# First product of a block of seven copied into a second PSUM bank, output projection's low halves on VectorE

## The chip, the cores and the metric

The kernel runs on one core of a Trainium2 chip. The metric is the device time of one execution, in microseconds, as the median of several. The engines are PE (TensorE, matrix products), DVE (VectorE), ACT (ScalarE), POOL (GpSimd) and SP (SyncE, which here only issues transfers). Each works through its own queue in order.

## The reference

Two layers of a trunk in which three branches run side by side on 640 tokens (512 sample, 128 prompt) of width 1024, with an adaptive modulation ahead of them. Cut to the part that the change touches:

```python
mod = jax.nn.silu(cvec) @ w_mod + b_mod
shift, scale, gate = jnp.split(mod[:, None, :], 3, axis=-1)
h = rms_norm(x, norm_g) * (1 + scale) + shift
... = jnp.split(h @ w_in, split_at, axis=-1)          # fu, fz and gl among them
...                                                   # o_r, o_m, o_f: retention, attention, Fourier
branches = jnp.stack([o_r * silu(rz), o_m * silu(mz), o_f * silu(fz)], axis=2)
proj = jnp.einsum('btnw,nwd->btnd', branches, w_branch)
merged = jnp.sum(proj * jax.nn.sigmoid(gl.reshape(B, T, N_BRANCH, D_MODEL)), axis=2)
x = x + gate * (merged @ w_out)
```

All inputs and outputs are float32.

## The kernel before

**Numbers.** Every float32 operand is split into a high half, rounded by a cast on ACT, and a low half, the difference, taken by DVE or POOL. A product is made of three passes on PE: high by high, low by high, high by low. `split` does this, and `low` (L74) is the subtraction; the casts are L78. Weights come by DMA into `raw` (L92, two buffers, issued by SP), and `wload` casts and splits them. The names are the same throughout: `wh`, `wl` for weights, `hh`, `hl` for the activations, `bq` for a branch's output.

**Layout.** Activations lie with channels in the partitions and the 640 tokens in the free dimension, in two halves `a` and `b` of 320. One matrix product covers 128 x 128 weights and 128 x 320 activations.

**The product phase** (`ph0`, `ph1`, once a layer) makes the gates and the branch products. Its unit is `seven`: a 2 x 2 block product (two channel blocks by two token halves) by seven products of sums instead of eight. It has three PSUM banks' worth of accumulators A, C and, for the third product, B. In the order of the code: product 0 into A; ACT copies A into SBUF (L1117); product 2 into B, and DVE adds copy and bank (L1113), which is the first half of the first result; product 1 on top of A, copied (L1125); product 4 into C; product 3 on top of A, copied (L1131), and C added; then `rest`, which is put off until the next block's first copy: product 5 on top of A, which is consumed by `last`, and product 6 into C. A product that goes on top of A waits for the copy of A before it. For a gate the results go through a tanh (ACT, L1241 for the last one, L1245 for the others); for a branch DVE multiplies them by (gate + 1) (L1258, L1263) and adds them to the running sum `mg` (L1265). There are 21 such blocks a layer: the Fourier branch's SiLU gate, three times four gates, and two times four branches; the middle branch uses `four`, a plain block product, instead.

**PSUM.** Of eight banks the phase uses six in rotation as `bank`, one (`fill`) for the modulation products, and one (`po`) for their transposes.

**Between the bank products** PE does modulation products for later (L187, `fill<-mraw`): their weights `mraw` come by DMA (L175), whose issue stands in ACT's queue. `bql`, the low-pass part of a branch output, comes back through memory (`ofd`), and is cast at L78.

**The output projection** (`px0`, `px1`) follows. The merged sum is cast to `hh` (L81) and its low half `hl` taken on DVE (L82). `w_out` comes in eight tiles d = 0 to 7 of 128 x 1024; the low halves of d = 0 are taken on DVE, of the others on POOL; tiles 4 to 7 are called `xwh`, `xwl`. DVE evacuates each output product from PSUM (L1349). In layer 1 PE then transposes it (L1357), and ACT squares it (L1360).

**What sets the order.** The tile scheduler places each engine's instructions by a simulated time line. So a few instructions less on one engine move rows on all the others.

Of the kernel before, what the change touches and what calls it, by code (L numbers as in the profile page):

```python
# [14 lines left out]
P = 128  # L15
D = 1024
NK = 8
# [13 lines left out]
def build(nc, tc, A, O):  # L31
# [24 lines left out]
        return psum["p"].tile([P, 512], F32, name="sm", tag="sm", bufs=psum["nsm"])  # L56

    def bank():
        return psum["p"].tile([P, 512], F32, name="bank", tag="bank", bufs=6)[:, :320]

    def fillp():
        return psum["p"].tile([P, 512], F32, name="fill", tag="fill", bufs=1)
# [1034 lines left out]
        while tail:  # L1097
            tail.pop(0)()

    def seven(ws, xs, y1, y2, last, done, tick):  # L1100
        a, b = HALF

        def product(ps, i, first):
            n = len(xs[i])
            for k in range(n):
                w = ws[i][0][:, k, :], ws[i][1][:, k, :]
                x = xs[i][k]
                for j, (u, v) in enumerate(PASSES):
                    PE.matmul(ps, w[u], x[v], start=(first and k == 0 and j == 0), stop=(k == n - 1 and j == 2),  # L1109
                              skip_group_check=True)  # L1110

        def add(o, v, ps):
            DVE.tensor_tensor(o, ps, v, op=ALU.add)  # L1113

        A = bank()
        product(A, 0, True)
        ACT.copy(y1[:, a], A)  # L1117
        tick(0)
        flush()
        B = bank()  # L1120
        product(B, 2, True)
        add(y1[:, a], y1[:, a], B)
        tick(1)
        product(A, 1, False)
        ACT.copy(y2[:, a], A)  # L1125
        tick(2)
        C = bank()
        product(C, 4, True)
        tick(3)
        product(A, 3, False)  # L1130
        ACT.copy(y2[:, b], A)  # L1131
        add(y2[:, b], y2[:, b], C)
        tick(4)

        def rest():
            product(A, 5, False)
            last(A)
            done(0)
            tick(5)
            product(C, 6, False)  # L1140
            add(y2[:, a], y2[:, a], C)
            done(1)
            tick(6)

        tail.append(rest)
# [41 lines left out]
    for l in range(DEPTH):  # L1187
# [26 lines left out]
        with ExitStack() as s:  # L1214
            gp = pool(s, f"ga{l}")
            psum["s"].close()
            psum_pool(f"ph{l}")
            fillp(), pout()
            blocks = [(0, b) for b in range(8, 12)] + [(1, b) for b in range(8)] if l == 0 else [(1, b) for b in range(8, 12)]
            steps = mod_steps(blocks, gp)  # L1220
            next(steps)
# [7 lines left out]
                fourier_gate(off, j + 2, m)  # L1229
                nc.sync.dma_start(ofd[:, j + 2, :], o)  # L1230

            seven(w0, hq, *zs, lambda ps: ACT.copy(zs[0][:, b], ps), fourier_done, lambda i: None)
            bql = rp2.tile([P, 4, TT], F32R, name="bql", tag="of", bufs=1)

            def merge(d0, d1, hs=slice(0, TT)):
# [3 lines left out]
            def gates(y2, n, bq, parts, np_):  # L1239
                def last(ps):  # L1240
                    ACT.activation(y2[0][:, b], ps, AF.Tanh, scale=0.5)  # L1241

                def fin(j):
                    y = y2[j][:, a] if j == 0 else y2[j]
                    ACT.activation(y, y, AF.Tanh, scale=0.5)  # L1245

                def tick(i):
                    if i in (3, 6):
                        next(steps, None)
                    if i % 2 and len(bq) < np_:  # L1250
                        with tc.issue_after(gated.ins):
                            bq.append(next(parts))

                return last, fin, tick

            def products(y2, n, ms, ps):
                def last(acc):
                    DVE.scalar_tensor_tensor(ps[0][:, b], y2[0][:, b], 1.0, acc, op0=ALU.add, op1=ALU.mult)  # L1258

                def fin(j):  # L1260
                    y, m, p = y2[j], ms[j], ps[j]
                    s_ = a if j == 0 else slice(0, TT)
                    DVE.scalar_tensor_tensor(p[:, s_], y[:, s_], 1.0, p[:, s_], op0=ALU.add, op1=ALU.mult)  # L1263
                    if n:
                        DVE.tensor_tensor(m, m, p, op=ALU.add)  # L1265
                def tick(i):
                    if i in (3, 6):
                        next(steps, None)

                return last, fin, tick  # L1270

            for n, (idx, src, tmp) in enumerate(((1, omt, None), (0, ort, om), (2, ort, om))):
                if n:
# [4 lines left out]
                for i in range(4):  # L1278
                    if n and i % 2 == 0:
                        y2 = tmp[2:4]  # L1280
                    else:
                        y2 = [fl.tile([P, TT], F32, name="tg", tag="th", bufs=2) for _ in range(2)]
                    seven(gl_weights(wgp, l, C_GL + D * idx + 256 * i), hq, *y2, *gates(y2, n, bq, parts, np_))
                    if n == 2 and i == 3:
                        merge(0, 4)
                    if i == 0:
# [8 lines left out]
                        ends = (lambda: merge(4, 6), lambda j, hs: merge(6 + j, 7 + j, hs)) if (n, i) == (2, 3) else ()  # L1295
                        four(br_plain(l, idx, 256 * i), bq, y2, ms, ps, lambda i: next(steps, None) if i else None, *ends)
                    else:
                        seven(br_weights(wgp, l, idx, 256 * i), bq, *ps, *products(y2, n, ms, ps))
            merge(4, 6)
            flush()  # L1300
            merge(6, NK)
# [5 lines left out]
        with ExitStack() as s:  # L1307
# [9 lines left out]
            ws = []  # L1317
            for d in range(NK):
                view = rows(A["w_out"][l], 0, NK, P * d, P)
                eng = DVE if d == 0 else POOL  # L1320
                if d < 4:
                    ws.append(wload(view, NK, P, eng))
                else:
                    rv = wraw(view, NK, P)
                    w = tuple(xp.tile([P, NK, P], F32R, name=n, tag=n, bufs=4) for n in ("xwh", "xwl"))
                    split(*w, rv, leng=eng)
                    ws.append(w)

            def out_mm(d, a, b):
# [130 lines left out]
```

## Time and profile before

| | |
|---|---|
| median of 3 runs | 1473.63 us (1472.76 to 1474.07) |
| profiled execution | 1475.04 us, span 1473.3 us |
| granted clock, mean | 0.993 |
| PE busy | 1411.6 us, 96% of the span |
| DVE busy | 1025.5 us, 70% |
| ACT busy | 756.2 us, 51% |
| POOL busy | 239.1 us, 16% |
| DMA | 138.91 MB, mean 94 GB/s |

The product phase of layer 0 lies from about 430 to 700 us of the span, that of layer 1 from about 1150 to 1410; the output projections follow each. Busy time is the sum of an engine's instructions; matrix products overlap, so that the mean of one (0.31 us) is longer than the time from one to the next. "Granted clock" is the share of full speed that TensorE was given. The chain of waits follows the span back from its end, at each step to what released it. A wait is put down to the releaser that came last.

### The profile page before, as it was taken

How to read it: one execution, taken by the hardware profiler on the slowest of the kernel's cores; microseconds unless marked ns; L12 is line 12 of the kernel's file. 1: busy time of each engine (PE TensorE's matmuls, PEld its weight loads, DVE VectorE, ACT ScalarE, POOL GpSimd, SP SyncE). 2: the span in 40 equal slices, each digit the busy share in tenths (PEclk: the TensorE clock that was granted, in tenths of full speed). 3: DMA queues.
4: the chain of work that ended last, by engine and by line, in shares of the span. 5: the costliest groups of instructions: out<-in, count | busy, mean ns of one | idle time of the engine just before them, and what ended most of it. 6: DMA issues, size and time to landing. Idle time of an engine off the chain costs nothing.

```text
span 1473.3 us, 25184 instructions
## 1 busy us (share of the span) xinstructions
PE 1411.6 (96%) x9793; PEld 1345.2 (91%) x9793; DVE 1025.5 (70%) x1896; ACT 756.2 (51%) x1607; POOL 239.1 (16%) x227
## 2 busy tenths in 40 slices
PE   6999999999999999999999999999999999999997
PEld 4989989988988989999999899899889899999997
DVE  5367776666887686698573777765759778779843
ACT  5546666544545453455354566664545445445542
POOL 1220000301102211122312100021110112112240
PEclk9999999999999999999999999999999999999999
DMA  9520003331325474233532100042222433323342
GB/s 317 179 76 1 15 16 98 102 84 33 94 90 176 130 221 129 57 85 92 166 101 84 33 15 16 15 138 77 73 73 65 146 108 104 94 80 86 90 125 87
DMA packets 175847, 138.91 MB, mean 94 GB/s; under 512 B 8304, under 2 KB 168688, under 8 KB 175728
## 3 DMA queue, kind: packets, MB, share of 16 engines
q1 hardware_dynamic: 157680, 120.16, 28.1%
q10 hardware_dynamic: 18048, 17.15, 3.7%
q8 instruction: 77, 1.26, 0.4%
q14 instruction: 42, 0.34, 0.1%
HBM read 125.98 MB, written 11.30 MB: 93 GB/s over the span
## 4 chain that ended last, share of the span: by engine, by line
PE 74%; DVE 12%; DMA 5%; ACT 4%; issue 4%; POOL 1%; SPq 0%; POOLq 0%; ACTq 0%; DVEq 0%
PE bank L1109 25%; PE sm L85 6%; PE sm L87 5%; PE sm L86 5%; PE big L269 4%; PE bank L1080 4%; PE big L513 4%; PE fill L319 3%; PE sm L319 3%; PE sm L534 2%; PE sm L526 2%; DVE wl L74 2%; PE fill L187 2%; DMA raw<-in_w_in 1%; PE big L411 1%
## 5 line engine op out<-in xcount | busy, mean ns | idle before, releaser
L74 DVE TENSOR_TENSOR wl<-raw,wh 128x1024 fp32r<-128x1024 f32 (+5 forms) x146 | 153.8, 1055 | 87.3 <-ACT wh L78 39.0
L78 ACT CAST wh<-raw 128x1024 fp32r<-128x1024 f32 (+5 forms) x126 | 104.7, 833 | 86.2 <-DMA raw<-in_w_in 27.9
L1109 PE MATMUL bank<-hh,wh 128*128 128x320 f32 x416 | 130.0, 315 | 5.5 <-ACT tg L1125 4.4
L85 PE MATMUL sm<-wh,hh 128*128 128x256 f32 (+2 forms) x456 | 134.2, 295 | 0.5 <-DVE vl L74 0.5
L86 PE MATMUL sm<-wl,hh 128*128 128x256 f32 (+2 forms) x456 | 133.8, 294 | 0.0
L87 PE MATMUL sm<-wh,hl 128*128 128x256 f32 (+2 forms) x456 | 132.6, 294 | 0.0
L1109 PE MATMUL bank<-hl,wh 128*128 128x320 f32 x416 | 128.6, 310 | 0.0
L1109 PE MATMUL bank<-hh,wl 128*128 128x320 f32 x416 | 127.1, 311 | 0.0
L74 POOL TENSOR_TENSOR wl<-raw,wh 128x1024 fp32r<-128x1024 f32 (+1 forms) x32 | 66.4, 2075 | 294.9 <-ACT wh L78 215.7
L74 POOL TENSOR_TENSOR wl<-st,wh 128x512 fp32r<-128x512 f32 x26 | 38.0, 1463 | 328.8 <-ACT wh L78 328.8
L85 PEld LDWEIGHTS sm<-wh,hh 128*128 128x128 f32 x456 | 87.8, 193 | 2.2 <-issue 0.8
L1109 PEld LDWEIGHTS bank<-hh,wh 128*128 128x128 f32 x416 | 78.3, 188 | 11.9 <-ACT tg L1125 5.2
L86 PEld LDWEIGHTS sm<-wl,hh 128*128 128x128 f32 x456 | 87.8, 193 | 0.1
L87 PEld LDWEIGHTS sm<-wh,hl 128*128 128x128 f32 x456 | 87.4, 192 | 0.4 <-issue 0.4
L1109 PEld LDWEIGHTS bank<-hl,wh 128*128 128x128 f32 x416 | 78.5, 189 | 0.0
L1109 PEld LDWEIGHTS bank<-hh,wl 128*128 128x128 f32 x416 | 78.0, 189 | 0.0
L74 DVE TENSOR_TENSOR ptl<-sm,pth 128x384 fp32r<-128x384 f32 x128 | 67.2, 549 | 13.9 <-ACT pth L78 12.9
L1109 PE MATMUL bank<-bq,wh 128*128 128x320 f32 x320 | 72.0, 311 | 0.0
L78 ACT CAST pth<-sm 128x384 fp32r<-128x384 f32 x128 | 57.2, 481 | 22.6 <-PE sm L526 21.8
L78 ACT CAST wh<-st 128x512 fp32r<-128x512 f32 x68 | 39.6, 618 | 55.1 <-PE bank L1109 53.7
L640 DVE TENSOR_REDUCE nm<-big 128x1 f32<-128x768 f32 x64 | 60.7, 948 | 1.7 <-PE big L513 1.6
L74 DVE TENSOR_TENSOR wl<-st,wh 128x512 fp32r<-128x512 f32 x42 | 40.8, 972 | 29.5 <-ACT wh L78 27.0
(578 smaller groups left out, 4540.3 us busy)
## 6 DMA issues: line engine op xcount, KB each, us to landing
raw<-in_w_in SPq DMA_DIRECT2D x96, 512.0 KB, 4.0
mraw<-in_w_mod ACTq DMA_DIRECT2D x32, 512.0 KB, 4.0
raw<-in_w_branch SPq DMA_DIRECT2D x24, 512.0 KB, 3.6
mraw<-in_w_mod SPq DMA_DIRECT2D x16, 512.0 KB, 9.2
raw<-in_w_out SPq DMA_DIRECT2D x16, 512.0 KB, 4.3
raw<-in_w_in SPq DMA_DIRECT2D x8, 384.0 KB, 6.1
om<-xd SPq DMA_DIRECT2D x16, 192.0 KB, 3.5
xd<-xt SPq DMA_DIRECT2D x8, 320.0 KB, 4.2
```

The source lines that it names most:

```text
L74: eng.tensor_tensor(lo, src, hi.bitcast(F32), op=ALU.subtract)
L78: ACT.copy(hi, src)
L85: PE.matmul(out, ah, bh, start=first, stop=False)
L86: PE.matmul(out, ah, bl, start=False, stop=False)
L87: return PE.matmul(out, al, bh, start=False, stop=last)
L187: PE.matmul(ps[c:c + 32, :n], cs[:, 2 * (j + i):2 * (j + i) + 32], rv[:, i, :], start=(j + i < 4), stop=(j + i >= 4), tile_position=(0, c))
L269: PE.matmul(ps[:, 512 * h:512 * h + 320], ws[a][:, k, :], xs[b][k][:, 320 * h:320 * h + 320], start=(first and k == 0 and i == 0), stop=(l ...
L319: PE.matmul(ps, w[a][:, k, :], (hh, hl)[b][k][:, hs], start=(k == 0 and i == 0), stop=(k == NK - 1 and i == 2))
L513: PE.matmul(S[:, 512 * h:512 * h + 384], qT[hd][a][:, t * P:(t + 1) * P], (kth, ktl)[b][hd % 3][:, 384 * h:384 * h + 384], start=(i == 0), ...
L640: DVE.tensor_reduce(nm, Sv, axis=AX.XY if len(Sv.shape) == 3 else AX.X, op=ALU.max, negate=True)
L1080: PE.matmul(A, ws[u][:, k, j * P:(j + 1) * P], xs[k][v][:, h, :], start=(k == 0 and i == 0), stop=(k == 3 and i == 2))
L1109: PE.matmul(ps, w[u], x[v], start=(first and k == 0 and j == 0), stop=(k == n - 1 and j == 2), skip_group_check=True)
```

## The change

In `seven`, product 0 is copied from its bank A into another PSUM bank, `pair`, instead of into SBUF. Product 2 is accumulated there on top of the copy, and `begin` consumes the bank: a tanh on ACT for a gate (L1252 after), a multiply on DVE for a branch (L1279 after), a copy into SBUF for the Fourier gate (L1240 after). The add on DVE is gone. The first two times in a phase that a `pair` bank is used, one product is written into it first (L1124 after; the code keeps count in `marked`); what it writes is overwritten by ACT's copy, on which product 2 then adds. The banks are divided anew: four `bank`, two `pair`. In the output projection all low halves of `w_out` are taken on DVE. Line numbers of the kernel after are 5 higher in the first part of the file, and more from `seven` on.

```diff
--- before.py
+++ after.py
@@ -56,7 +56,12 @@
         return psum["p"].tile([P, 512], F32, name="sm", tag="sm", bufs=psum["nsm"])
 
     def bank():
-        return psum["p"].tile([P, 512], F32, name="bank", tag="bank", bufs=6)[:, :320]
+        return psum["p"].tile([P, 512], F32, name="bank", tag="bank", bufs=4)[:, :320]
+
+    marked = []
+
+    def pair():
+        return psum["p"].tile([P, 512], F32, name="pair", tag="pair", bufs=2)[:, :320]
 
     def fillp():
         return psum["p"].tile([P, 512], F32, name="fill", tag="fill", bufs=1)
@@ -1097,7 +1102,7 @@
         while tail:
             tail.pop(0)()
 
-    def seven(ws, xs, y1, y2, last, done, tick):
+    def seven(ws, xs, y2, begin, last, done, tick):
         a, b = HALF
 
         def product(ps, i, first):
@@ -1114,12 +1119,14 @@
 
         A = bank()
         product(A, 0, True)
-        ACT.copy(y1[:, a], A)
+        B = pair()
+        if len(marked) < 2:
+            marked.append(PE.matmul(B, ws[0][0][:, 0, :], xs[0][0][0], start=True, stop=True))
+        ACT.copy(B, A)
         tick(0)
         flush()
-        B = bank()
-        product(B, 2, True)
-        add(y1[:, a], y1[:, a], B)
+        product(B, 2, False)
+        begin(B)
         tick(1)
         product(A, 1, False)
         ACT.copy(y2[:, a], A)
@@ -1216,6 +1223,7 @@
             psum["s"].close()
             psum_pool(f"ph{l}")
             fillp(), pout()
+            marked.clear()
             blocks = [(0, b) for b in range(8, 12)] + [(1, b) for b in range(8)] if l == 0 else [(1, b) for b in range(8, 12)]
             steps = mod_steps(blocks, gp)
             next(steps)
@@ -1229,7 +1237,7 @@
                 fourier_gate(off, j + 2, m)
                 nc.sync.dma_start(ofd[:, j + 2, :], o)
 
-            seven(w0, hq, *zs, lambda ps: ACT.copy(zs[0][:, b], ps), fourier_done, lambda i: None)
+            seven(w0, hq, zs[1], lambda ps: ACT.copy(zs[0][:, a], ps), lambda ps: ACT.copy(zs[0][:, b], ps), fourier_done, lambda i: None)
             bql = rp2.tile([P, 4, TT], F32R, name="bql", tag="of", bufs=1)
 
             def merge(d0, d1, hs=slice(0, TT)):
@@ -1240,9 +1248,12 @@
                 def last(ps):
                     ACT.activation(y2[0][:, b], ps, AF.Tanh, scale=0.5)
 
+                def begin(ps):
+                    ACT.activation(y2[0][:, a], ps, AF.Tanh, scale=0.5)
+
                 def fin(j):
-                    y = y2[j][:, a] if j == 0 else y2[j]
-                    ACT.activation(y, y, AF.Tanh, scale=0.5)
+                    if j:
+                        ACT.activation(y2[j], y2[j], AF.Tanh, scale=0.5)
 
                 def tick(i):
                     if i in (3, 6):
@@ -1251,7 +1262,7 @@
                         with tc.issue_after(gated.ins):
                             bq.append(next(parts))
 
-                return last, fin, tick
+                return begin, last, fin, tick
 
             def products(y2, n, ms, ps):
                 def last(acc):
@@ -1259,15 +1270,19 @@
 
                 def fin(j):
                     y, m, p = y2[j], ms[j], ps[j]
-                    s_ = a if j == 0 else slice(0, TT)
-                    DVE.scalar_tensor_tensor(p[:, s_], y[:, s_], 1.0, p[:, s_], op0=ALU.add, op1=ALU.mult)
+                    if j:
+                        DVE.scalar_tensor_tensor(p, y, 1.0, p, op0=ALU.add, op1=ALU.mult)
                     if n:
                         DVE.tensor_tensor(m, m, p, op=ALU.add)
+
+                def begin(acc):
+                    DVE.scalar_tensor_tensor(ps[0][:, a], y2[0][:, a], 1.0, acc, op0=ALU.add, op1=ALU.mult)
+
                 def tick(i):
                     if i in (3, 6):
                         next(steps, None)
 
-                return last, fin, tick
+                return begin, last, fin, tick
 
             for n, (idx, src, tmp) in enumerate(((1, omt, None), (0, ort, om), (2, ort, om))):
                 if n:
@@ -1280,7 +1295,7 @@
                         y2 = tmp[2:4]
                     else:
                         y2 = [fl.tile([P, TT], F32, name="tg", tag="th", bufs=2) for _ in range(2)]
-                    seven(gl_weights(wgp, l, C_GL + D * idx + 256 * i), hq, *y2, *gates(y2, n, bq, parts, np_))
+                    seven(gl_weights(wgp, l, C_GL + D * idx + 256 * i), hq, y2[1], *gates(y2, n, bq, parts, np_))
                     if n == 2 and i == 3:
                         merge(0, 4)
                     if i == 0:
@@ -1295,7 +1310,7 @@
                         ends = (lambda: merge(4, 6), lambda j, hs: merge(6 + j, 7 + j, hs)) if (n, i) == (2, 3) else ()
                         four(br_plain(l, idx, 256 * i), bq, y2, ms, ps, lambda i: next(steps, None) if i else None, *ends)
                     else:
-                        seven(br_weights(wgp, l, idx, 256 * i), bq, *ps, *products(y2, n, ms, ps))
+                        seven(br_weights(wgp, l, idx, 256 * i), bq, ps[1], *products(y2, n, ms, ps))
             merge(4, 6)
             flush()
             merge(6, NK)
@@ -1317,13 +1332,12 @@
             ws = []
             for d in range(NK):
                 view = rows(A["w_out"][l], 0, NK, P * d, P)
-                eng = DVE if d == 0 else POOL
                 if d < 4:
-                    ws.append(wload(view, NK, P, eng))
+                    ws.append(wload(view, NK, P, DVE))
                 else:
                     rv = wraw(view, NK, P)
                     w = tuple(xp.tile([P, NK, P], F32R, name=n, tag=n, bufs=4) for n in ("xwh", "xwl"))
-                    split(*w, rv, leng=eng)
+                    split(*w, rv, leng=DVE)
                     ws.append(w)
 
             def out_mm(d, a, b):
```

ACT, start of layer 0's product phase; `mg0` and `mg1` are the Fourier gate's halves, `tg` a gate's buffer, `mraw` modulation weights. Before:

```order
L1117 COPY tg_5223<-bank_5253 128x320
L78 CAST w40_5245<-raw2_5227 128x512
L175 DMA mraw_5543<-in_w_mod 128x4x256
L1117 COPY mg0_5123<-bank_5438 128x320
L1227 ACTIVATE mg1_5124<-tg_5143 128x640
L1245 ACTIVATE tg_5223<-tg_5223 128x320
L175 DMA mraw_5594<-in_w_mod 128x4x256
L192 COPY mraw_5468<-fill_5470 128x256
L1125 COPY tg_5224<-bank_5253 128x320
L1125 COPY mg1_5124<-bank_5438 128x320
L175 DMA mraw_5670<-in_w_mod 128x4x256
L175 DMA mraw_5703<-in_w_mod 128x4x256
```

After:

```order
L180 DMA mraw_5544<-in_w_mod 128x4x256
L83 CAST wh_5424<-raw_5420 128x256
L83 CAST wh_5424<-raw_5420 128x512
L1240 COPY tg_5142<-bank_5144 128x320
L1235 ACTIVATE mg0_5123<-tg_5142 128x640
L83 CAST w40_5246<-raw2_5228 128x512
L1235 ACTIVATE mg1_5124<-tg_5143 128x640
L1252 ACTIVATE tg_5224<-pair_5267 128x320
L180 DMA mraw_5594<-in_w_mod 128x4x256
L1125 COPY pair_5446<-bank_5439 128x320
L1132 COPY tg_5225<-bank_5254 128x320
L197 COPY mraw_5469<-fill_5471 128x256
```

The issue of the second load of modulation weights shown before (`mraw_5543`, `mraw_5544` after) stood behind the copy of `bank_5253`, and stands ahead of both tanh of `mg` now. The copies into `tg` and `mg0` are copies into `pair`, and a tanh that reads `pair_5267` stands ahead of the second.

PE, where `bql` is first used in layer 0. Before:

```order
L1109 MATMUL bank<-bq_5218,wh 128x320
L1109 MATMUL bank<-bq_5217,wl 128x320
L1109 MATMUL bank<-bql,wh 128x320 x2
L187 MATMUL fill<-mraw,cs 32x256 x3
L1109 MATMUL bank<-hh_149,wh 128x320
L1109 MATMUL bank<-hl_157,wh 128x320
```

After:

```order
L1114 MATMUL bank<-hh_152,wh 128x320
L1114 MATMUL bank<-hl_160,wh 128x320
L1114 MATMUL bank<-hh_152,wl 128x320
L1114 MATMUL bank<-bql,wh 128x320 x2
L192 MATMUL fill<-mraw,cs 32x256
L1114 MATMUL bank<-bql,wl 128x320
L1114 MATMUL bank<-bql,wh 128x320 x2
L1114 MATMUL bank<-bql,wl 128x320
L192 MATMUL fill<-mraw,cs 32x256 x2
L1114 MATMUL pair<-bq_5218,wh 128x320
```

The products with `bql` stood right behind those with `bq`. Now the twelve products with `hh` and `hl` that followed them stand ahead of them (the last three are shown), and product 2 into `pair` follows.

DVE, end of layer 0's product phase and start of the output projection; `hl_163` and `hl_164` are the last low halves of the merged sum. Before:

```order
L1113 TENSOR_TENSOR om<-bank,om 128x320
L1113 TENSOR_TENSOR tg<-bank,tg 128x320
L1258 SCALAR_TENSOR_TENSOR om<-tg,bank 128x320
L1265 TENSOR_TENSOR mg_5129<-mg_5129,om 128x640
L1113 TENSOR_TENSOR om<-bank,om 128x320
L1263 SCALAR_TENSOR_TENSOR om<-tg,om 128x640
L82 SCALAR_TENSOR_TENSOR hl_163<-mg_5129,hh_155 128x640
L1265 TENSOR_TENSOR mg_5130<-mg_5130,om 128x640
L82 SCALAR_TENSOR_TENSOR hl_164<-mg_5130,hh_156 128x640
```

After:

```order
L79 TENSOR_TENSOR wl<-raw,wh 128x1024
L1269 SCALAR_TENSOR_TENSOR om<-tg,bank 128x320
L1118 TENSOR_TENSOR om<-bank,om 128x320
L1276 TENSOR_TENSOR mg_5129<-mg_5129,om 128x640
L1274 SCALAR_TENSOR_TENSOR om<-tg,om 128x640
L79 TENSOR_TENSOR wl<-raw,wh 128x1024
L1276 TENSOR_TENSOR mg_5130<-mg_5130,om 128x640
L87 SCALAR_TENSOR_TENSOR hl_163<-mg_5129,hh_155 128x640
L87 SCALAR_TENSOR_TENSOR hl_164<-mg_5130,hh_156 128x640
L79 TENSOR_TENSOR xwl<-raw,xwh 128x1024 x2
```

Two low halves of `w_out` (`wl`) stand among the last steps of the merged sum (a third one a little earlier), and those of tiles 4 and 5 (`xwl`) right behind the last `hl`, ahead of the evacuations.

## Rows read from the trace of the kernel before

**Rows 1.** The page, busy us of each engine, share and instructions

```profile
PE 1411.6 (96%) x9793; PEld 1345.2 (91%) x9793; DVE 1025.5 (70%) x1896; ACT 756.2 (51%) x1607; POOL 239.1 (16%) x227
```

**Rows 2.** Windows of the phase: length, then busy us (instructions) by engine, clock, DMA

```profile
480.00:500.00 20.00, 20.00 (x150) 18.19 (x149) 14.14 (x23) 9.82 (x19) 4.47 (x3) 1.00 0.47 141
620.00:640.00 20.00, 20.00 (x138) 19.86 (x136) 19.32 (x30) 11.95 (x24) 6.30 (x3) 1.00 0.30 79
```

**Rows 3.** Chain of waits, layer 1's phase: start us, us, what

```profile
1323.28 68.51 PE bank L1109 x467
```

**Rows 4.** Waits of PE, 425 to 700 us: total us, times, longest

```profile
PE bank L1109 <- ACT bql L78: 1.8, 1, 1.8
PE fill L187 <- DMA mraw<-in_w_mod: 1.5, 1, 1.5
PE bank L1109 <- ACT tg L1125: 1.3, 1, 1.3
PE bank L1109 <- ACT tg L1131: 0.6, 1, 0.6
```

**Rows 5.** Waits of PE, 1145 to 1402 us

```profile
PE bank L1109 <- ACT tg L1125: 3.1, 2, 2.2
PE fill L187 <- DMA mraw<-in_w_mod: 2.0, 1, 2.0
```

**Rows 6.** Waits of PE, 690 to 770 us

```profile
PE sm L86 <- DVE hl L82: 0.7, 1, 0.7
```

**Rows 7.** Instructions of L1113 and L1117 (ns), L74 by form (busy us, mean ns)

```profile
L1113 DVE TENSOR_TENSOR tg<-bank,tg x54: 472/481/492, 438.0 to 1399.8; 128x320 f32<-128x320 f32 x54
L1117 ACT COPY tg<-bank x18: 407/427/431, 430.5 to 1382.6; 128x320 f32<-128x320 f32 x18
L74 DVE TENSOR_TENSOR wl<-raw,wh 128x1024 fp32r<-128x1024 f32 x29 | 35.4, 1220 | 27.2 <-ACT wh L1033 18.4 <-ACT wh L1043 7.8 <-ACT wh L78 0.8
```

**Rows 8.** Chain of waits, start of layer 0's phase

```profile
442.62 0.61 PE fill L187 x8
455.54 7.31 DMA ofd<-of
486.35 1.00 PE fill L187 x16
```

**Rows 9.** Time line of ACT: start us, us, instruction, idle before it

```profile
451.37 0.43 ACT L1117 COPY tg<-bank 128x320 f32<-128x320 f32 x1 [2.91 <-DVE mg L1228]
451.38 0.37 ACTq L175 DMA_DIRECT2D mraw<-in_w_mod  x1
```

**Rows 10.** Chain of waits, start of layer 1's phase

```profile
1176.46 7.26 DMA mraw<-in_w_mod
```

**Rows 11.** Windows at the start of layer 1's phase, columns as in rows 2

```profile
1160.00:1162.00 2.00, 1.15 (x7) 1.15 (x8) 2.00 (x4) 0.80 (x2) 0.00 (x0) 0.91 0.00 0
1162.00:1164.00 2.00, 2.00 (x9) 1.92 (x8) 1.19 (x3) 0.44 (x1) 0.00 (x0) 0.50 0.00 0
1164.00:1166.00 2.00, 2.00 (x20) 0.91 (x19) 1.36 (x2) 2.00 (x5) 0.47 (x1) 0.74 0.00 0
```

**Rows 12.** Chain of waits, end of layer 0's phase

```profile
696.98 2.96 DVE mg L1265
703.54 2.15 DVE hl L82
```

**Rows 13.** Time line of POOL, then of DVE, at the same place

```profile
696.85 2.40 POOL L74 TENSOR_TENSOR wl<-raw,wh 128x1024 fp32r<-128x1024 f32 x1 [0.21 <-ACT wh L78]
701.91 0.82 DVE L1265 TENSOR_TENSOR mg<-mg,om 128x640 f32<-128x640 f32 x1
```

**Rows 14.** Windows at the same place, columns as in rows 2

```profile
695.00:700.00 5.00, 5.00 (x33) 5.00 (x32) 4.16 (x5) 1.72 (x3) 4.04 (x2) 1.00 0.36 108
700.00:705.00 5.00, 5.00 (x28) 4.44 (x26) 4.09 (x5) 2.49 (x3) 2.84 (x1) 1.00 0.68 203
```

## The prediction

> **What bounds the kernel now.** I read the page's busy shares first [rows 1]: PE 96%, the next engine 70%. Then the windows of the long product phase [rows 2]: in all ten stretches of 20 us from 480 to 680 us PE is busy 20.00 us (two of the rows stand), even where VectorE has 19.32. The chain of waits says the same: one unbroken run of 467 bank products takes 68.51 us, 0.147 us each [rows 3]. So in these stretches an instruction taken off VectorE or ScalarE is worth nothing, and one added on PE costs its whole length. What can be gained stands only where PE waits, and the views of PE's waits list it: in layer 0's phase four waits, 1.8, 1.5, 1.3 and 0.6 us [rows 4]; in layer 1's 3.1 and 2.0 [rows 5] and the same 0.6 again (its row is word for word that of layer 0, one stands); and one of 0.7 at each output projection, for the low half `hl` of the merged sum [rows 6] (either layer has this row, one stands). Together 12.3 us, under 1% of the time.
>
> **The change part by part, against the profiled run's 1475.04 us (span 1473.3; the run is 1.41 us above the median of 1473.63).**
>
> *The first sum.* There are 42 uses of `seven`, 21 a layer. Each loses one VectorE add of 0.481 us [rows 7]: 42 x 0.481 = 20.2 us of VectorE. Its copy stays, one for one, but now goes into PSUM; the trace has no copy that ends there. From below, I bound it by nothing but the order (it could be free), from above by the 0.427 us of the copy into SBUF [rows 7] plus one more such copy; I take 0.427. The tanh or multiply that read `y` reads the bank instead, same shape. By saturation the 20.2 us are worth nothing, except where VectorE stands on a path to a wait of PE.
>
> [...]
>
> *The price on PE.* Four marking products (two a layer) of a bank product's length: 4 x 0.147 = 0.6 us. The order of PE has 35 runs of modulation products between the bank products (28 and 7 by layer) where it had 29 (23 and 6). What such a switch costs is in the chain of waits: 8 of them in one run take 0.61 us, 16 take 1.00 [rows 8], so two runs of 8 cost 0.22 more than one of 16. Six more: 1.3 us.
>
> *The new wait.* The third product of a `seven` now accumulates on the copy and must wait for it. Before, only the second did, and far later. What stands between the end of the first product and the third is, in the order of PE, 12 to 27 bank products nearly everywhere (12 x 0.147 = 1.8 us, four times the copy), 8 in three places, and 4 modulation rows or fewer in three. PE's queue is in order, so what is late there delays every product behind it. The nearest thing that the trace shows is the copies of the second and fourth product, which gate PE in the same way: 84 of them, and they cost 1.3 + 0.6 + 3.1 + 0.6 = 5.6 us of PE's waits [rows 4, 5]. Half as many new ones would by that cost 2.8; the other bound is nothing. Since 3 of 42 have nearly no cover, about 0.4 us each, I take 1.4.
>
> *Start of the phase, layer 0.* Two of the four waits follow from ScalarE's queue. The copy of the first product into `tg` sat idle 2.91 us until VectorE's `mg` freed the buffer, and the load of the next modulation weights stands right behind it in ScalarE's queue, issued at 451.38 [rows 9]. In the new order that load stands ahead of the tanh that has the same wait. Its data ended the wait of 1.5 us [rows 4]. The 1.8 us wait is for `bql`, whose data come back through memory, 7.31 us from 455.54 [rows 8]; its first use on PE moves behind 12 more bank products, 1.76 us. So of 3.3 us all could go. Against it: both transfers share the queues with weight loads, and in the order of SP the store of `of` now stands behind a load of input weights. Between nothing and 3.3 I take 2.3. The wait of 1.3 us for the copy of `tg` stays: it hangs on VectorE's `bq`, on which the change does nothing.
>
> *Start of the phase, layer 1.* The 2.0 us wait is a modulation load again, issued at 1176.46 and landing after 7.26 us [rows 10]. By the same order it goes out earlier: between 0 and 2.0, taken 1.5. The 3.1 us of `tg` are two waits: 2.2 of them at the phase's start, behind the rotation and the adds on VectorE, where TensorE's clock then fell as well: granted 0.91, 0.50 and 0.74 in three stretches of 2 us [rows 11], so 0.18 + 1.0 + 0.52 = 1.7 us more. Two products that were not there before now stand in front of this gap, so it gets narrower by less than half a microsecond, and I count nothing of it, nor of the clock. The second, 0.9, comes after a chain on which VectorE's adds lie; half, 0.4, goes.
>
> *End of the phase and output projection.* PE waits 0.6 for the copy L1131 [rows 4] in either layer. The order of PE now puts 17 products between where it had 10, so 1.0 us more cover: gone. Behind it VectorE's `mg` takes 2.96 us at 696.98 and `hl` 2.15 at 703.54 [rows 12], while POOL runs a low half of 2.40 us at 696.85, and then another; the same `mg` takes 0.82 at 701.91 [rows 13]. With POOL's low halves gone and 0.82 for either, 2.14 and 1.33 us come back; three low halves at 1.22 [rows 7], 3.66 us, are put on VectorE in this stretch. VectorE is 4.16 and 4.09 of 5 busy there [rows 14]: 8.25 - 3.47 + 3.66 = 8.4 of 10. It fits, and the last `hl` comes out 1 to 2 us earlier than 703.54 + 2.15. Its wait of 0.7 goes. Both layers: 2 x (0.6 + 0.7) = 2.6. The bounds are 0 and 2.6; since the cover has moved by more than the waits, I take 2.6. The last four low halves a layer stand ahead of the evacuations of the output products: 2 x 1.22 on VectorE ahead of the first. Its bank is wanted again by the fourth output product, which comes after two others of 24 products each; by columns one of these takes 24 x 0.147 x 384/320 = 4.2 us, an estimate from rows 3. With most of both done early, one stands as cover: 4.2 - 2.44 leaves 1.8. I allow 0.3.
>
> [...]
>
> *Sum.* Gained 2.3 + 1.5 + 0.4 + 2.6 = 6.8. Lost 0.6 + 1.3 + 1.4 + 0.3 = 3.6. Net 3.2: 1475.04 - 3.2 = 1471.8 for a run like the profiled one, less 1.41, **1470.4 us** as a median.
>
> **Rivals.** (a) *No measurable change.* The transfers land no earlier, because they wait for the same queues; both starts give nothing. Then 3.0 gained, 3.6 lost: 1473.63 + 0.6 = 1474.2. For it: the two waits for memory are those of 7.3 us, not of queue position. Against: the row of 2.91 us of idle ScalarE right ahead of the issue.
>
> (b) *Slower: the new wait decides.* ScalarE is in order, and what stands ahead of a copy there may itself wait for VectorE. The one such row is 2.91 us long [rows 9]. A copy caught behind it comes 2.91 + 0.43 = 3.3 us after its product, against 14 products of cover, 2.06 us: 1.3 us of PE lost each time. If 9 of the 42 are caught, that is 11.7 in place of the 1.4 that I took: 1470.4 + 10.3 = 1480.7. It decides from the point where these waits sum to more than 1.4 + 3.2 + 2.95 = 7.6 us, six such places. For it: the tanh of a gate, which waits for VectorE to free its buffer, stands ahead of copies in ScalarE's new order. Against: of 84 copies with the same duty five cost PE anything [rows 4, 5].
>
> (c) *More than I count.* VectorE's relief of 0.481 us a `seven` reaches the starts too, and the waits of 1.3 and 2.2 and the fallen clock's 1.7 go with the rest: 1.0 + 0.5 + 0.5 (what I left of the others) + 5.2 = 7.2 more, 1463.2. For it: VectorE is busy through both gaps. Against: the chain there is `bq`, not the adds.
>
> (d) *The clock falls in layer 0 as in layer 1*, if PE's pauses join up there: 1.7 us [rows 11], 1472.1. [...] Here the clock is 1.00 in the windows listed [rows 2], and fell after one pause only; at each of 42 places it would cost 71 us, for which I have under one chance in a hundred, held in (b)'s.
>
> **How the numbers follow.** Forecast 0.40; (c) 0.10; (a) 0.31; (d) 0.05; (b) 0.14. A measurement of this kernel tells 0.2%, 2.95 us, from no change: faster is below 1470.7, slower above 1476.6. The forecast stands just inside faster; what of it falls above 1470.7 is balanced by what of (a) falls below. So faster 0.50, same 0.36, slower 0.14. The range: from (c), 1463.5, to 0.4 above the edge of slower, 1477.0, which leaves out most of (b). The forecast's own range, by its bounds, is 1467.5 to 1473.
>
> **What would show it.** Right: in the phases PE's waits for `bql` and for `mraw` are shorter or gone; no wait for L1131 nor for `hl`; `mg` near 0.82 us at the phase's end; PE's busy windows still 20.00. Each of these terms is read off one row. Wrong: PE rows waiting for the copy into `pair`, more than a microsecond or two in all; waits for an evacuation in the output projection; a lower granted clock at the start of layer 0's phase; or new loads of modulation weights landing late all the same.

## The result: 0.6% slower

The changed kernel takes 1480.95 us in the median of five runs (1479.05 to 1483.58), the kernel before 1472.76 (1468.82 to 1474.07): a ratio of 1.0062, 95% interval 1.0047 to 1.0078. Forecast were 1470.4, in 1463.5 to 1477.0. The profiled run after is 1480.95 us, its span 1479.2, against 1473.3.

On the page of the changed kernel PE's busy time has grown by 7.7 us [rows 1], though only four products were added:

```profile
PE 1419.3 (96%) x9797; PEld 1347.6 (91%) x9797; DVE 1018.4 (69%) x1868; ACT 758.9 (51%) x1609; POOL 210.7 (14%) x213
```

By the first and last bank product, layer 0's phase lasts 272.20 us where it lasted 268.45, layer 1's 256.94 where it lasted 253.04; all the rest of the span became 1.7 us shorter. So 3.75 + 3.90 - 1.73 = 5.9 us, the difference of the two spans, and the loss is in the phases. PE's waits in layer 0's (425 to 710 us) are now:

```profile
PE bank L1114 <- ACT tg L1132: 1.8, 1, 1.8
PE bank L1114 <- DVE wl L79: 1.0, 1, 1.0
PE bank L1114 <- DVE tg L1118: 0.4, 1, 0.4
PE fill L192 <- DMA mraw<-in_w_mod: 0.4, 1, 0.4
```

The 1.8 us for `bql` and the 0.6 for the copy before the end are gone, that for `mraw` fell from 1.5 to 0.4 [rows 4]. The wait for the copy of `tg` grew from 1.3 to 1.8, and two for VectorE are new. Layer 1 (1145 to 1410 us):

```profile
PE bank L1114 <- DVE wl L79: 2.1, 3, 0.9
PE bank L1114 <- ACT tg L1132: 1.8, 1, 1.8
PE bank L1085 <- DVE om L1091: 0.8, 1, 0.8
PE bank L1114 <- ACT tg L1138: 0.5, 1, 0.5
PE bank L1114 <- ACT wh L1048: 0.5, 1, 0.5
PE bank L1114 <- DVE tg L1118: 0.4, 1, 0.4
PE pair L1114 <- ACT pair L1125: 0.2, 1, 0.2
```

The 2.0 us for `mraw` are gone [rows 5], and in their place PE waits in many small pieces for low halves of weights, for casts and for a sum. On the last row stands all that the view lists of PE's waiting for the new copy: 0.2 us. The output projection of layer 0, where `hl` had cost 0.7 [rows 6], now waits 1.1 for an evacuation:

```profile
PE sm L90 <- DVE or L1363: 1.1, 1, 1.1
```

And the line of the new copy (ns: least, median, most; then who waited for it):

```profile
L1125 ACT COPY pair<-bank x42: 410/412/437, 430.2 to 1398.0; 128x320 f32<-128x320 f32 x42
...
  PE pair L1114: 0.2, 1
```

At 0.412 us it is 0.015 shorter than the copy into SBUF, 0.427 [rows 7], and 0.004 to 0.016 shorter than the lines of the changed kernel that copy the same 128x320 from a bank into SBUF (medians 0.416 to 0.428). VectorE at the end of layer 0's phase (time line: start us, us, instruction):

```profile
703.66 0.82 DVE L1276 TENSOR_TENSOR mg<-mg,om 128x640 f32<-128x640 f32 x1
...
707.00 1.72 DVE L87 SCALAR_TENSOR_TENSOR hl<-mg,hh 128x640 fp32r<-128x640 f32 x2
708.84 1.23 DVE L79 TENSOR_TENSOR xwl<-raw,xwh 128x1024 fp32r<-128x1024 f32 x1
```

`mg` takes 0.82 us where it took 2.96 with GpSimd at work [rows 12], two `hl` together 1.72, and the `xwl` behind them stands ahead of the evacuations. So that part went as forecast, but for the evacuation's wait.

**Where PE's busy time grew.** PE's time line of the changed kernel at 500 us:

```profile
499.58 0.50 PE L201 MATMUL po<-sel,mraw 128*128 128x2 f32 x4
500.01 0.62 PE L192 MATMUL fill<-mraw,cs 128*32 128x256 f32 x2
500.56 0.41 PE L1114 MATMUL bank<-bq,wl 128*128 128x320 f32 x1
...
501.35 0.62 PE L192 MATMUL fill<-mraw,cs 128*32 128x256 f32 x2
501.89 0.41 PE L1114 MATMUL bank<-hh,wh 128*128 128x320 f32 x1
```

The trace has two records a modulation product (192 in layer 0's phase for its 96), so `x2` is one product of a group of four, standing by itself; it holds PE from 500.01 to 500.56, 0.55 us, and the next 0.54. A whole group, `x8`, took 0.61 us before [rows 8], and where one stands alone, as at 455.58, it is 0.57 from its start to the next bank product. The first records of its four products start 0.007 us apart there and last 0.38 to 0.40: they run beside one another, and a piece costs nearly what a group costs. This is the largest item between the two profiles: all intervals that begin or end at a modulation product, less waits, sum to 25.6 us in layer 0's phase where they summed to 21.0. That is 4.5, more than the phase's growth of 3.75; its waits became shorter. In the order of PE 28 runs stand there with 12 incomplete groups, where 23 with 5 stood. (A run is what stands between two bank products; the incomplete groups are the pieces of up to four that the runs are made of, less the 24 whole groups that there are.) In layer 1 these intervals, waits with them, are equal (8.7 and 8.75 us), and it is the time from bank product to bank product that grew, from 242.3 to 246.2 us. One of its waits, on the chain (start us, us, what):

```profile
1340.66 4.42 PE bank L1114 x30
...
1346.76 1.31 DVE raw L1029
...
1348.47 0.68 DVE raw L1030
...
1351.22 2.25 DVE wl L79
```

and on the time line of three engines:

```profile
1350.83 1.54 POOL L79 TENSOR_TENSOR w<-raw,w 128x512 fp32r<-128x512 f32 x1 [2.83 <-ACT w L83]
1351.14 2.31 DVE L79 TENSOR_TENSOR wl<-raw,wh 128x1024 fp32r<-128x1024 f32 x1
1353.51 0.41 PE L1114 MATMUL bank<-hq1h,wl 128*128 128x320 f32 x1 [0.94 <-DVE wl L79]
```

VectorE subtracts the low half `wl` only at 1351.1, behind the sums of weights (L1029, L1030) and other work. It then takes 2.31 us, with a subtraction of GpSimd beside it, where the mean before was 1.22 [rows 7]; those 1.1 us are more than the wait. At the same block before, PE ran without a pause. It is one of the three such waits of layer 1, 0.9 us.

A stop costs more than its listed wait. Here the product at 1353.51 starts 1.25 us after the one before it, and the next one 0.25 us after that, where 0.147 is the pace [rows 3]: 1.2 us lost for 0.9 listed. I count as a stop a bank product that starts more than 0.19 us behind another and that some engine released. Layer 1's phase then has 13 stops that cost 7.5 us; before it had 3 that cost 4.4. The difference, 3.1 us, is most of the 3.9 by which the phase grew. All three of before were for ScalarE's copies. Of the 13, eight are for VectorE (5.2 us), though VectorE had been relieved of 10 us of adds there.

### The profile page after: what moved, and what is told of

It is laid out like the page before. It is cut to its first block, busy times and chain, and to the rows that moved or that the text cites. A ratio compares the mean times of both kernels' runs of the same rounds, so it can differ in the third digit from the quotient of the medians.

```text
span 1479.2 us, 25156 instructions
## 1 busy us (share of the span) xinstructions
PE 1419.3 (96%) x9797; PEld 1347.6 (91%) x9797; DVE 1018.4 (69%) x1868; ACT 758.9 (51%) x1609; POOL 210.7 (14%) x213
## 4 chain that ended last, share of the span: by engine, by line
PE 71%; DVE 13%; DMA 5%; issue 5%; ACT 4%; POOL 1%; SPq 0%; ACTq 0%; POOLq 0%; DVEq 0%
PE bank L1114 19%; PE sm L90 6%; PE sm L92 5%; PE sm L91 5%; PE big L274 4%; PE big L518 4%; PE bank L1085 4%; PE pair L1114 4%; PE fill L324 3%; PE sm L324 3%; DVE wl L79 3%; PE sm L539 2%; PE fill L192 2%; PE sm L531 2%; DMA raw<-in_w_out 2%
## 5 line engine op out<-in xcount | busy, mean ns | idle before, releaser
L79 DVE TENSOR_TENSOR wl<-raw,wh 128x1024 fp32r<-128x1024 f32 (+5 forms) x152 | 165.2, 1091 | 91.4 <-ACT wh L1038 44.4
L1114 PE MATMUL bank<-hh,wh 128*128 128x320 f32 x312 | 98.7, 316 | 4.1 <-ACT tg L1132 3.6
L1114 PE MATMUL bank<-hh,wl 128*128 128x320 f32 x312 | 96.9, 311 | 0.0
L1114 PE MATMUL bank<-hl,wh 128*128 128x320 f32 x312 | 96.8, 310 | 0.0
L79 POOL TENSOR_TENSOR wl<-raw,wh 128x512 fp32r<-128x512 f32 (+1 forms) x26 | 49.6, 1909 | 274.5 <-ACT wh L83 187.9
L1114 PEld LDWEIGHTS bank<-hh,wh 128*128 128x128 f32 x312 | 58.9, 189 | 9.8 <-ACT tg L1132 4.6
L1114 PEld LDWEIGHTS bank<-hl,wh 128*128 128x128 f32 x312 | 59.0, 189 | 0.0
L1114 PEld LDWEIGHTS bank<-hh,wl 128*128 128x128 f32 x312 | 59.0, 189 | 0.0
L531 PE MATMUL sm<-ident,pt 128*128 128x128 f32 x384 | 57.8, 273 | 1.2 <-DVE ptl L79 1.0
```

The costliest lines, as they stand in the source:

```text
L79: eng.tensor_tensor(lo, src, hi.bitcast(F32), op=ALU.subtract)
L531: PE.transpose(tp_[:, c * P:(c + 1) * P], pt[:, kt * P:(kt + 1) * P], ident)
```

## The experiments

All are timed in rounds beside the kernel before on the same chip; ratios are to it, with their 95% interval. Two theories were tested. Theory 1: broken groups of modulation products. Theory 2: product 2 lost its freedom. For theory 2 the two orders of PE were compared: before, product 2 of a `seven` starts ahead of the end of product 0 in 16 of 42 blocks, right behind it in 23, behind one or two modulation products in 2, and 12 bank products behind in one. After, it starts 12 products or more behind in 36 of 42 and never ahead.

**Which half of the change.** One kernel has the pair bank alone, with

```diff
-                    ws.append(wload(view, NK, P, DVE))
+                    ws.append(wload(view, NK, P, DVE if d == 0 else POOL))
```

(and the same for `xwl`), one the output projection alone.

> The pair bank in seven as in the changed kernel, the output projection's low halves back on POOL. Theory 1 (the time went into PE's modulation products, which the new order breaks into 28 runs and 12 incomplete groups of four in layer 0 instead of 23 and 5, and into new waits of layer 1's phase): this kernel has the same 28 and 7 runs as the changed one, so it stays within 2 us of the changed kernel, 1479 to 1483. Rival (the low halves on VectorE cost it: the wait of 1.1 us for an evacuation and rows pushed late): it comes back by more than 3 us, to under 1478.

> Only the output projection's low halves moved to VectorE, seven as before. Theory 1: its runs of modulation products are as before but for one (23 and 7), so it is within 2 us of the kernel before, 1471 to 1475, and the waits for hl of 0.7 us are gone. Rival (the low halves on VectorE cost it): slower than before by 3 us or more.

Measured: 1480.94 us, 1.0067 (1.0041 to 1.0094), and 1470.03 us, 0.9989 (0.9976 to 1.0003). The pair bank carries the whole loss. The low halves on VectorE make no difference that can be told; of all kernels tried theirs is the fastest, and its interval just includes the kernel before. PE's waits for `hl` are gone in it, and stand at 0.8 and 1.0 us in the other.

**Groups kept together by a critical section** around the loop of L187, in the changed kernel and in that before.

> The changed kernel with each group of four modulation products kept together (a critical section around them). Runs 23 and 8 instead of 28 and 7, no incomplete groups instead of 12 and 2. Theory 1: a run costs about 0.5 us (0.09 before, 0.30 and 0.10 behind it), an incomplete group 0.22, so (28 - 23) x 0.5 + 12 x 0.22 = 5.1 us come back in layer 0 and nothing in layer 1: 1475 to 1477, nearer the kernel before than the changed one. Rival (the new waits for copies and low halves are what costs): no more than 2 us come back, 1479 or above.

> The kernel before with each group of four modulation products kept together: 24 and 8 runs instead of 23 and 6, no incomplete groups instead of 5 and 1. Theory 1: 3 more runs x 0.5 less 6 x 0.22 = 0.2 us, no change within 2 us, 1471 to 1475. Rival (keeping the groups together saves or costs something by itself, whatever the runs): over 3 us to either side.

Measured: 1587.03 us (1.0773) and 1597.85 (1.0857). The section itself costs over 100 us, and they say nothing on either theory. The priority does the same without it:

```diff
+        with tc.high_priority():
             for i in range(kk):
                 c = 32 * ((j + i) % 4)
                 PE.matmul(ps[c:c + 32, :n], cs[...], rv[:, i, :], ...)
```

> The changed kernel, with the modulation products given priority in the scheduler, so that each group of four stands together: 21 and 6 runs in the two phases (one group more outside of each), no incomplete group, instead of 28 and 7 runs with 12 and 2 incomplete groups. At 0.5 us a run and 0.22 a group (estimates from the two traces) that is 6 x 0.5 + 14 x 0.22 = 6 us less: about 1475, 1473 to 1477. Rival (the new waits carry the loss): 1479 or more.

> The kernel before with the same priority: 21 and 5 runs instead of 23 and 6, no incomplete groups instead of 5 and 1. By the same prices 1.8 us less, within 3 us of the kernel before: 1469 to 1473. Rival (the priority itself moves the time, by early products): outside of that by more than 3 us.

Measured: 1483.84 us, 1.0085 (1.0068 to 1.0102), and 1475.06, 1.0018 (1.0002 to 1.0033). Not what theory 1 expects. The phases did get shorter, 268.2 and 252.7 us in the changed kernel, 4 us each; but the first eight products now ran ahead of the phase, which by itself shortens it, and there PE stood for their data and the phase began 4.8 us later. PE's waits of the first:

```profile
PE fill L193 <- DMA mraw<-in_w_mod: 3.2, 2, 1.8
PE fill L193 <- issue: 2.9, 1, 2.9
```

So the edit was confounded, and was tried again with the priority from the third unit on (`if first > 1`):

> The changed kernel with priority for the modulation products but for the first eight of a phase, so that none runs ahead of the phase as in the run before this one: 23 and 7 runs, no incomplete groups, instead of 28 and 7 with 12 and 2. Theory 1 (broken modulation products): 5 x 0.5 + 14 x 0.22 = 5.6 us back, about 1475. Theory 2 (product 2 may no longer stand right behind product 0, where the order of before has it in most blocks, and what is put between is missing elsewhere): little back, 1479 or more.

> The kernel before with the same: 22 and 7 runs, no incomplete groups instead of 5 and 1. Theory 1: 1.3 us less, 1470 to 1472. Theory 2 says nothing of it.

Measured: 1476.38 us, 1.0040 (1.0027 to 1.0052), and 1478.18, 1.0050 (1.0030 to 1.0071). In the changed kernel 4.6 us come back by the medians, 3.2 by the ratios (1.0062 to 1.0040), where theory 1 expects 5.6 of 8.2; the rest stays. By the traces the time at modulation products in layer 0 fell from 25.6 to 19.1 us, but PE's stops there cost 5.8 us instead of 2.9, and the phase got only 2.6 us shorter. Layer 1's got 3.4 us shorter, though it had only two incomplete groups to lose; half of that may be clock: its fall there costs the changed kernel about 0.2 + 1.0 + 0.5 = 1.7 us, an estimate from the clock of 0.90, 0.50 and 0.75 in three windows of 2 us (they stand in the next section). The kernel before got no faster, but slower. Its granted clock explains most of that (last section).

**The opposite: more breaks.** `tc.high_priority(offset=150)` in the kernel before.

> The kernel before with a lesser priority for the modulation products, which happens to break them up: 42 and 11 runs, 18 and 3 incomplete groups, banks and dependences as before. Theory 1: 24 runs x 0.5 and 15 groups x 0.22 more, 15 us, about 1487. Theory 2: breaking them costs little, under 5 us more than before, below 1477.

Measured: 1489.77 us, 1.0120 (1.0101 to 1.0138): 18 us, where 15 were expected. Its time line shows the pieces one by one:

```profile
433.90 0.60 PE L188 MATMUL fill<-mraw,cs 128*32 128x256 f32 x2
434.44 0.41 PE L1110 MATMUL bank<-hh,wl 128*128 128x320 f32 x1
434.78 0.62 PE L188 MATMUL fill<-mraw,cs 128*32 128x256 f32 x2
435.33 0.42 PE L1110 MATMUL bank<-hh,wh 128*128 128x320 f32 x1
```

From one such piece to the next it is 0.88 us with one bank product of 0.147 between, so a piece and its switches cost 0.73. In layer 0 the time at modulation products is 35.4 us, 14.4 more than before, and the phase is 11.4 us longer. So theory 1's price holds where groups are broken.

**The banks alone.** First, four and two banks, the third product in the two, with the add kept; then five of six in one rotation.

```diff
-        B = bank()
+        B = pair()
         product(B, 2, True)
```

> The kernel before with the PSUM banks divided as in the changed one (four and two, the third product's accumulator in the two), and nothing else: the copy still goes to SBUF and the add stays on VectorE, so no product waits for a new copy. 28 and 8 runs with 11 and 3 incomplete groups. Theory 1 (the division of the banks lets the scheduler's order break the modulation products): 7 x 0.5 + 8 x 0.22 = 5.3 us slower than before, 1476 to 1479. Rival (the new dependence on the copy costs): no slower than before, within 2 us.

> The kernel before with five banks in the rotation instead of six, one left unused, and nothing else. Product 2 is as free as before of the copy, but 29 and 8 runs, 9 and 2 incomplete groups. Theory 1 and the loss by fewer banks: 8 x 0.5 + 5 x 0.22 = 5.1 us slower, 1475 to 1479. Theory 2 alone: no change, within 2 us.

Measured: 1487.59 us, 1.0103 (1.0086 to 1.0120), and 1485.71, 1.0095 (1.0077 to 1.0113). Each is slower than the whole change. One bank less in the rotation costs 14 us, of which theory 1 expects 5. One of PE's waits in layer 0's phase of the latter shows part of the rest:

```profile
PE bank L1109 <- DVE tg L1113: 3.2, 1, 3.2
```

These 3.2 us for VectorE's add to free a bank stand once in each layer; before there is none. In the kernel with four and two banks product 2 starts ahead of product 0's end in 37 blocks and right behind it in the other 5, freer than before. With five banks it starts ahead or right behind in 32, and 12 products or more behind in 8. Either way the time at modulation products in layer 0 is as in the changed kernel, 25.6 and 24.9 us.

**The dependence alone.** The changed kernel with `pair()` returning the next of six shared banks; and the kernel before with a dependence of product 2 on the copy that it doesn't need.

```diff
-        ACT.copy(y1[:, a], A)
+        held = ACT.copy(y1[:, a], A)
...
+                    if held is not None:
+                        tc.add_manual_dep(ins.ins, held.ins.name, ...)
```

> The changed kernel with the six banks in one rotation again: the copy goes into the next of the six, the third product accumulates on it and waits for it as in the changed kernel, the low halves of the output projection are on VectorE. 19 and 5 runs, 2 and 0 incomplete groups. Theory 1: 5 runs x 0.5 and 4 groups x 0.22 less than before, 3.4 us, and the waits for bql and hl gone: 1466 to 1471. Rival (the new dependence on the copy costs): near the changed kernel, 1478 or more.

> The kernel before with one thing more: product 2 waits for ScalarE's copy of product 0, by a dependence that it doesn't need. Banks, copy into SBUF, adds on VectorE and the low halves on GpSimd as before. 21 and 5 runs, 4 and 0 incomplete groups. Theory 2: slower by 5 us or more, 1477 to 1482, near the changed kernel. Theory 1: 3 runs x 0.5 and 2 groups less, 1469 to 1472.

Measured: 1479.31 us, 1.0051 (1.0037 to 1.0066), and 1486.89, 1.0104 (1.0086 to 1.0121). Both have fewer runs of modulation products than before (19 and 21 in layer 0, 18.2 and 19.7 us), and are slower: theory 1 is not enough. That holding product 2 costs, as theory 2 says, fits both; each also has a new order throughout, which is tested below. PE's waits in layer 1 of the held kernel:

```profile
PE bank L1109 <- DVE mg L1116: 4.7, 3, 1.8
PE bank L1109 <- ACT om L1120: 2.2, 2, 1.7
PE bank L1109 <- ACT tg L1120: 1.7, 4, 0.5
```

The copies (L1120 there) cost PE 3.9 us here, and VectorE's sums 4.7; in layer 0 the copies cost 2.9 more. So here about half of the price stands at the new wait itself. In the kernel with shared banks the chain shows one such copy:

```profile
1324.13 4.19 PE bank L1114 x29
1328.31 0.52 ACT wh L83
1328.83 0.33 ACT tg L1249
1329.16 0.51 ACT w L83
1329.67 0.02 ACT bql L83
1329.69 0.61 issue
1330.30 0.43 ACT bank L1125
1330.73 0.04 issue
1330.77 1.29 PE bank L1114 x7
```

ScalarE first does a cast, a tanh and two more casts (the 0.61 called issue is the rest of that of `bql`); the copy comes at 1330.30. PE's last product ends at 1329.41, and PE stands 1.37 us for the copy. That is the mechanism of rival (b), ScalarE's order ahead of the copy, though behind its own work and not behind VectorE.

**A new order and no dependence.** The four marking products in the kernel before:

> The kernel before with only the four marking products added: each is written into the third product's bank, which that product then overwrites. No new dependence on the copy. 22 and 6 runs, 4 and 1 incomplete groups; product 2 still starts ahead of the end of product 0 or right behind it in 38 of 42 blocks. Theory 2 (the freedom of product 2 is what is lost): 4 x 0.147 = 0.6 us, no change within 2 us, 1470 to 1474. Rival (any new order costs what was measured): 4 us or more slower.

Measured: 1477.58 us, 1.0042 (1.0028 to 1.0056). Forecast were 0.6 us, and 6.1 came: the rival holds. Its granted clock was 0.9901 in the mean of the runs, against 0.9923 in the runs of the kernel before beside it; times clock it is 1462.8 against 1460.4, only 2.4 more. So most of it is the clock, but that belongs to the new order too: in layer 0's phase PE stood 2.2 us for `mraw` up to 461.14, and the clock fell; in the kernel before it stood 1.5 there, and the clock did not fall (windows of the kernel before, then of this one, columns as in rows 2):

```profile
460.00:470.00 10.00, 8.19 (x57) 7.34 (x54) 7.03 (x10) 5.10 (x10) 1.86 (x2) 1.00 0.32 112
460.00:470.00 10.00, 6.97 (x36) 6.20 (x37) 5.96 (x9) 3.59 (x8) 1.81 (x1) 0.66 0.34 118
```

So a new order can cost 6 us with product 2 nearly as free as before (ahead of product 0's end or right behind it in 36 blocks, and in four more with only the marking product between). Of the kernels tried but for those of the critical section, all with another order, one was not slower, the others by 3 to 18 us.

## Why the prediction was wrong

**The step that failed** is the side of the losses: the new wait (1.4 us) was priced at its own place only, the division of the banks had no term, and the switches (1.3 us) were too small. The phases, where all three stand, became 7.65 us longer, and PE's wait for the new copy was 0.2 of it.

**The new wait.** I looked at what stands between product 0 and product 2 in the new order, found 12 to 27 products, and took the wait as covered at 1.4 us. The waiting for the copy was indeed covered: 0.2 us. But the cover is not free. Before, product 2 had its weights in the tile of product 0's, needed nothing from ScalarE, and in 41 of 42 blocks no other bank product stood between the end of product 0 and its start. The order of before shows that, and I did not look. Made to wait, it leaves that place to others, and PE stops for those: in layer 1 for low halves, casts and sums, 7.5 us of stops instead of 4.4. Holding product 2 alone costs 15 us, with shared banks and the changed sums 7.5. That it was a filler whose loss makes these stops is argued from the orders, not shown by itself.

**A term that was left out**: the division of the banks. I priced no bank. One bank less costs 14 us, the division alone 16. The broken modulation products of layer 0 go with it and not with the wait: with fewer banks and product 2 free they take 25.6 and 24.9 us, as in the changed kernel (25.6), and with six banks and product 2 held 19.7 and 18.2, less than before (21.0).

**A term mis-sized**: switches to modulation products, 1.3 us by runs; 4.5 by the trace, since I counted runs and not the incomplete groups. I also read `x8` of rows 8 as eight products, where it is one group of four, each with two records; that hid that one product alone costs nearly what four do (0.55 us against 0.57 to 0.61).

**What was right**: `bql`, `mraw`, the copy before the end and `hl` gave back what was said of them, 1.8 + 1.1 + 2.0 + 0.6 + 1.4 = 6.9 by their waits against 6.4 in the sum (2.3 + 1.5 + 2.6); in layer 1 0.5 of the copy's 0.6 came back as the wait for L1138. Of layer 1's 3.1 us for the copy of `tg` 1.3 went, where I had counted 0.4; in layer 0 0.5 came on top. VectorE's 20.2 us bought nothing that a row shows: PE's waits for VectorE in the phases went from none to 1.4 and 3.3 us. The evacuation took 1.1 instead of 0.3, in layer 0. Rival (d) did not come: the clock in layer 0 stayed 1.00, and in layer 1 it fell as before [rows 11]:

```profile
1162.00:1164.00 2.00, 0.93 (x5) 0.93 (x6) 2.00 (x3) 1.65 (x5) 1.48 (x1) 0.90 0.79 258
1164.00:1166.00 2.00, 2.00 (x9) 2.00 (x8) 1.93 (x4) 0.02 (x1) 0.00 (x0) 0.50 0.00 1
1166.00:1168.00 2.00, 2.00 (x12) 2.00 (x12) 0.94 (x2) 1.36 (x2) 0.00 (x0) 0.75 0.00 0
```

Rival (b) had the price (1480.7), not the place: the copies into `pair` held PE by no more than 0.2 us in the changed kernel. They did hold it in the kernel with shared banks (1.4 us once) and in the held one (up to 1.7).

**What stays open.** The parts don't add: held alone 15 us, divided alone 16, both together, without the add, 8. Perhaps a product that must wait needs fewer banks at a time; that was not tried. Each of these kernels also has another order throughout, and a new order costs by itself, so the share of each cause in the 8.2 us is not known. The nearest to it are the changed kernel's own traces: 4.5 us more at modulation products in layer 0, 3.1 more in stops in layer 1. With whole groups 3 to 5 of the 8.2 came back, part of it perhaps clock.

## What to carry to other kernels

When an operation on a saturated engine is given a new operand, ask first what it was doing before: if the old order could place it freely, part of the price can be paid elsewhere than at the new wait (here 0.2 us stood at it). Count accumulators like engines: taking a bank out of a rotation cost 14 us here, while 20 us less of VectorE bought nothing. And judge an edit in a scheduled kernel by the whole new order of the bound engine, old against new, not by the rows around the edit.

## What was not expected of the hardware

A part of the scatter of the times is TensorE's granted clock. In the twelve runs of the kernel before that stood beside the last two kernels, 1468.59 us went with a clock of 0.994, and 1476.46 with 0.989; multiplied, 1459.8 and 1460.2. All twelve products lie between 1459.2 and 1462.2. It isn't so everywhere: beside the four kernels tried after the critical section, the times of the kernel before run from 1468.72 to 1476.26, and the products from 1457.5 to 1465.9, no narrower. So a difference of a few us between kernels can be, but need not be, a pause of PE after which the clock fell, as in the windows above (0.90, 0.50 and 0.75 over 6 us in the changed kernel's layer 1, 0.66 over 10 us with the marking products). By this product the kernel before with whole groups is at 1461.9 in the median, the plain one beside it at 1461.2 (clock 0.9893 against 0.9928), and 2.4 us apart by the means: most of its 7 us is the clock. The losses named above stay: the changed kernel 1470.2, held 1474.3, five banks 1472.3, divided 1476.7, broken groups 1475.0, the pair bank alone 1470.7, each against 1459.8 to 1461.3.
